# A decoder block on one core: two pooling groups by halves of the tokens, and a pooled half of the output projection, beside the last pair of heads

## The chip, the core and the metric

One core of a Trainium2 chip runs the whole kernel in one launch. TensorE (PE) multiplies, with its weight loads as a queue of their own (PEld); VectorE (DVE), ScalarE (ACT) and GpSimd (POOL) do the elementwise work; SyncE (SP) issues most DMAs. The metric is the device time in microseconds, median of several runs; smaller is better.

## The reference, cut to what matters

One layer over 1024 tokens of width 1024, in float32:

```python
h = x @ w_in                              # [pool 512 | q 512 | k 512 | v 512 | forget gate 8]
# pool: channel group g (128 channels, g = 0..3), windows 2, 4, 8, 16
d = trailing_mean(u, window[g]) - u       # fewer tokens at the start
pool = (d @ pool_w[g]) * pool_scale
# attention: 8 heads of 64, causal, bias c_t - c_s with c = cumsum(log sigmoid(f))
attn = softmax(q k^T / 8 + c_t - c_s) v
x = LayerNorm(alpha * x + concat(pool, attn) @ w_out)
x = LayerNorm(alpha * x + relu(x @ w_mlp1)**2 @ w_mlp2)
```

## The kernel before

Every float32 matrix product is made of three matmuls of rounded parts: each operand is split into a rounded high part (a CAST on ScalarE) and the rest (a subtraction on VectorE); `three` issues high x high (L83), high x low (L84) and low x high (L85). `split` (L71, L72) makes the parts, `load_w` loads a 128-column block of weights and splits it.

The order of the work on each engine comes from a scheduler: the program is written as generators, and the scheduler orders the instructions of each engine by its own estimates, within the written dependencies; tile pools with a fixed number of buffers per tag ("S" 3, "U" 2, "B" 14, "Q" 10, "A" 9 in SBUF; "s" 3, "pt" 2, "pv" 1, "mm" 2 banks of PSUM) release and hand on buffers. Each engine and each DMA queue then works in order.

The stages around the change:

- Values and gates, then the pooling groups. `pool_group` projects one group of 128 channels for all 1024 tokens: for each half of the tokens (`c`, 512 wide) 8 blocks of x by `three`, 24 matmuls; the window sums by doubling on VectorE over 1024 columns, the difference `d`, its split. `pool_linear` multiplies by the group's 128 x 128 matrix (3 matmuls for each half), scales on ScalarE and stores to `mix_dram`. Groups 3, 2 and 1 (`EARLY`) run so before the attention.
- Attention, four pairs of heads, 8 blocks a pair. A block of 256 queries (`m` = 0 to 3) of one head: `att_probs` makes the scores (L370, L371, and L373 for the mask in the last pair), VectorE adds the gate row and takes the running minimum (L376), ScalarE the exponential (L378). `att_values`, one block later, transposes (L398), splits (L399 on ScalarE, L400 on VectorE) and multiplies with V (L414). L419 and L420 take the result out, to `mix_dram`; `row_scales` stores the reciprocal row sums to `rin_dram`.
- Filler: `fillstep`, called between the blocks, runs pieces of a generator at a rate. For the first three pairs that is the next pair's projection of q and k; for the last pair it is `last_fill`: group 0 whole.
- The output projection. `wo` holds `w_out` in 8 blocks of 128 rows: three are loaded and split here, five were split earlier and lie in `wo_dram`. For each 256 tokens (`m`) the mixture is read back from `mix_dram` in two halves, the pooled one (channel blocks 0 to 3) and the attention one (4 to 7, multiplied with the row scales), and split. For each tile of 128 tokens `t` 48 matmuls of 512 columns (8 blocks, 2 halves of the output, `three`), then the norm and the transposes for the MLP.
- The MLP, from about 400 us to the end, which the change leaves alone.

```python
fill.update(gen=gen, credit=0.0, rate=pieces / over)   # pieces of a generator over `over` calls of fillstep
```

## Time and profile before

| | us |
|---|---|
| median of 3 runs | 1043.03 |
| lowest and highest run | 1040.76, 1044.09 |
| span of the profiled execution, first to last instruction | 1039.2 |
| PE busy | 1016.9 (98%) |
| weight loads (PEld) busy | 844.9 (81%) |
| VectorE busy | 760.8 (73%) |
| ScalarE busy | 510.7 (49%) |
| GpSimd busy | 142.7 (14%) |

The profile has the span of one execution and no time of its own for it; the median of the runs is 3.8 us above the span. A busy PE is the union of pipelined matmuls: one of 512 columns is shown 0.39 us long, though the next starts 0.23 us after it. The granted TensorE clock is full over the whole span.

### The profile page before, as it was taken

Reading aid. Unit: us, or ns where it says so; the run is one execution under the profiler, and the core shown is the slowest. Engines: PE = TensorE matmul, PEld = TensorE weight load, DVE = VectorE, ACT = ScalarE, POOL = GpSimd, SP = SyncE. Lnnn points to the kernel's source line nnn. Section 1 sums busy time; section 2 is a strip of 40 time slices with the busy share of each in tenths; the row PEclk is TensorE's granted clock in tenths of the full one; section 3 lists DMA queues with packets and bytes.
Section 4 is the critical chain, followed back from the end, with each engine's and each line's share of the span. In section 5 each row is a group of like instructions: output and inputs, shape, how many; then the busy total and the mean of one; then the engine's idle time right before and its main releaser. Section 6 shows DMA issues by size and latency. Waiting matters only on the chain.

```text
span 1039.2 us, 14092 instructions
## 1 busy us (share of the span) xinstructions
PE 1016.9 (98%) x4976; PEld 844.9 (81%) x4976; DVE 760.8 (73%) x1303; ACT 510.7 (49%) x820; POOL 142.7 (14%) x246
## 2 busy tenths in 40 slices
PE   9999999999989999999999999999999999999996
PEld 9988888878777888887888888888788888888884
DVE  4776678777786887988878778788875566566547
ACT  4623566666673321676766766768531221122152
POOL 0200112111000021113122122120100000000057
PEclk9999999999999999999999999999999999999998
DMA  9702211111376642139667566566999888878753
GB/s 358 274 27 87 98 52 52 34 50 54 101 250 207 195 148 102 62 134 349 266 240 276 215 262 263 227 231 221 346 308 305 283 264 281 271 228 271 242 186 121
DMA packets 114678, 206.29 MB, mean 199 GB/s; under 512 B 9576, under 2 KB 77992, under 8 KB 114608
## 3 DMA queue, kind: packets, MB, share of 16 engines
q1 hardware_dynamic: 96896, 141.82, 41.1%
q0 software_dynamic: 17280, 62.92, 15.6%
q8 instruction: 39, 0.64, 0.2%
q10 hardware_dynamic: 432, 0.66, 0.2%
q14 instruction: 31, 0.25, 0.1%
HBM read 132.42 MB, written 72.94 MB: 198 GB/s over the span
## 4 chain that ended last, share of the span: by engine, by line
PE 50%; issue 4%; DVE 3%; DMA 1%; POOL 1%; SPq 0%; ACT 0%; DVEq 0%; POOLq 0%
PE s L981 15%; PE pv L981 8%; PE s L627 8%; PE mm L627 6%; PE pt L627 6%; PE pv L627 4%; PE pt L981 2%; PE mm L981 2%; DMA hid_dram<-A 1%; DMA A<-hid_dram 1%; DVE B L72 1%; POOL hid_dram L752 0%; POOL A L620 0%; SPq L960 0%; DVE A L750 0%
## 5 line engine op out<-in xcount | busy, mean ns | idle before, releaser
L71 ACT CAST B<-S 128x1024 fp32r<-128x1024 f32 (+1 forms) x79 | 69.0, 885 | 168.8 <-DMA S<-in_w_dram 61.2
L627 PE MATMUL s<-B,Q 128*128 128x512 f32 x480 | 113.5, 389 | 0.2 <-ACT B L71 0.2
L627 PEld LDWEIGHTS s<-B,Q 128*128 128x128 f32 x480 | 90.0, 188 | 19.3 <-ACT B L71 0.6
L72 DVE TENSOR_TENSOR B<-S,B 128x1024 fp32r<-128x1024 f32 (+1 forms) x79 | 79.4, 1013 | 29.9 <-ACT B L71 29.8
L981 PE MATMUL s<-B,Q 128*128 128x512 f32 x390 | 94.8, 389 | 0.0
L71 ACT CAST Q<-S 128x1024 fp32r<-128x1024 f32 x52 | 54.7, 1052 | 64.0 <-PE s L627 17.0
L981 PEld LDWEIGHTS s<-B,Q 128*128 128x128 f32 x390 | 73.2, 188 | 15.6
L981 PE MATMUL s<-B,A 128*128 128x512 f32 x333 | 83.1, 394 | 1.2 <-DMA A<-hid_dram 1.2
L752 POOL DMA_DIRECT2D hid_dram<-A x90 | 48.3, 542 | 217.1 <-ACT A L749 174.7
L981 PEld LDWEIGHTS s<-B,A 128*128 128x128 f32 x333 | 62.4, 188 | 15.9 <-DMA A<-hid_dram 1.9
L72 DVE TENSOR_TENSOR Q<-S,Q 128x1024 fp32r<-128x1024 f32 x52 | 63.4, 1219 | 15.6 <-ACT Q L71 15.5
L627 PE MATMUL pt<-B,Q 128*128 128x512 f32 x300 | 71.6, 389 | 0.0
L627 PE MATMUL mm<-B,Q 128*128 128x512 f32 x300 | 71.6, 389 | 0.0
L414 PE MATMUL pv<-A,B 128*128 128x256 f32 x320 | 64.0, 299 | 3.0 <-DVE A L400 1.6
L627 PEld LDWEIGHTS mm<-B,Q 128*128 128x128 f32 x300 | 56.3, 188 | 11.7
L627 PEld LDWEIGHTS pt<-B,Q 128*128 128x128 f32 x300 | 56.3, 188 | 11.7
L414 PEld LDWEIGHTS pv<-A,B 128*128 128x128 f32 x320 | 49.6, 188 | 19.0 <-ACT A L399 8.8
L400 DVE TENSOR_TENSOR A<-pt,A 128x512 fp32r<-128x512 f32 (+1 forms) x80 | 49.2, 634 | 18.2 <-ACT A L399 17.7
L378 ACT ACTIVATE A<-A,nm 128x1024 f32<-128x1024 f32 (+7 forms) x64 | 49.8, 778 | 20.0 <-DVE nm L376 19.6
L750 DVE TENSOR_TENSOR A<-A,A 128x1024 f32<-128x1024 f32 x45 | 53.6, 1220 | 0.0
L399 ACT CAST A<-pt 128x512 fp32r<-128x512 f32 (+1 forms) x80 | 41.7, 540 | 18.5 <-PE pt L398 17.3
L981 PE MATMUL pv<-B,Q 128*128 128x512 f32 x204 | 50.3, 390 | 0.0
(407 smaller groups left out, 2309.7 us busy)
## 6 DMA issues: line engine op xcount, KB each, us to landing
hid_dram<-A POOLq DMA_DIRECT2D x105, 512.0 KB, 4.0
S<-in_w_dram SPq DMA_DIRECT2D x62, 512.0 KB, 3.7
Q<-hid_dram SPq DMA_DIRECT2D x101, 256.0 KB, 5.1
A<-hid_dram SPq DMA_DIRECT2D x79, 256.0 KB, 4.5
S<-in_wuqk_dram SPq DMA_DIRECT2D x12, 512.0 KB, 3.3
wo_dram<-Q POOLq DMA_DIRECT2D x10, 512.0 KB, 4.0
B<-wo_dram SPq DMA_DIRECT2D x10, 512.0 KB, 4.1
A<-ncf_dram SPq DMA_DIRECT2D x8, 512.0 KB, 3.9
```

The source lines that it names most:

```text
L71: nc.scalar.copy(hi, src)
L72: nc.vector.tensor_tensor(lo, src, hi.bitcast(F32), ALU.subtract)
L378: nc.scalar.activation(pt[:, :nk], pt[:, :nk], AF.Exp, bias=nm, scale=-1.0, accum_out=rsum[h][:, i : i + 1])
L399: nc.scalar.copy(tt[:, 0, ev], tp[:, ev])
L400: nc.vector.tensor_tensor(tt[:, 1, ev], tp[:, ev], tt[:, 0, ev].bitcast(F32), ALU.subtract)
L414: nc.tensor.matmul(ov, V[j][:, h].rearrange("p s d -> p (s d)"), tt[:, s, a:b], start=(j == 0 and s == 0), stop=(j == 2 * m + 1 and s == 1),)
L627: nc.tensor.matmul(dst, b[x][:, k], A[a][y][:, k], start=first and k == 0 and i == 0, stop=k == H - 1 and i == 2, skip_group_check=not first,)
L750: nc.vector.tensor_tensor(x, x, hi.bitcast(F32), ALU.subtract)
L752: nc.gpsimd.dma_start(hid_dram[self.u, :, i, AT[name] : AT[name] + 2 * CH], part.rearrange("p q n t -> p (q n t)"))
L981: nc.tensor.matmul(dst, h[:, p_], w[q_], start=first and u == self.us[0] and j == 0, stop=u == self.us[-1] and j == 2, skip_group_check=no ...
```

## The change

`EARLY` loses group 1, which joins group 0 in the filler of the last pair, now by halves of the tokens: `late_group(g, c, w)` projects 512 tokens, copies them out on ScalarE, forms the window sum on GpSimd (group 0: a subtraction of neighbours; group 1: an addition of neighbours, a scale-and-add on VectorE, another addition, and a few columns at the seams) and splits the result. The factor 1/window moves into the scale. `late_linear(g, c)` mixes and stores one half; it loads and splits the group's matrix each time. The filler then loads the output weights in two lots, reads the pooled half of the first mixture back and begins the output projection of token tile 0 with its 24 matmuls of blocks 0 to 3. It is 44 pieces over 24 steps, before 18 over 14. The output projection finishes what has been begun.

```diff
-EARLY, LATE = (3, 2, 1), (0,)
+EARLY, LATE = (3, 2), (1, 0)
...
+    def late_group(g, c, w):
+        x = slot("Q", [2, CH], F32)
+        u, s = x[:, 0], x[:, 1]
+        dst = bank("mm")
+        for _ in proj(dst, c, w):
+            yield
+        nc.scalar.copy(u, dst)
+        add = nc.gpsimd.tensor_tensor
...
+        if g == 0:
+            d, mx = s, u
...
+            add(d[:, 1:], u[:, :-1], u[:, 1:], ALU.subtract)
+        else:
+            d, mx = u, s
+            add(s[:, 1:], u[:, 1:], u[:, :-1], ALU.add)
...
+            nc.vector.scalar_tensor_tensor(d, u, -4.0, s, ALU.mult, ALU.add)
+            add(d[:, 2:], d[:, 2:], s[:, :-2], ALU.add)
...
+        y = slot("Q", [2, CH])
+        split(y[:, 0], y[:, 1], d)
+        pooled[g, c] = (y, mx)
+
+    def late_linear(g, c):
+        st = slot("S", [P], F32)
+        nc.sync.dma_start(st, poolw[:, g])
+        pw = slot("U", [2, P])
+        split(pw[:, 0], pw[:, 1], st)
+        y, mx = pooled.pop((g, c))
+        dst = bank("mm")
+        three(dst, (pw[:, 0], pw[:, 1]), (y[:, 0], y[:, 1]), True, True)
+        nc.scalar.activation(mx, dst, AF.Copy, scale=scales[:, g : g + 1])
+        nc.sync.dma_start(mix_dram[2 * c : 2 * c + 2, :, g, :]..., mx...)
...
     def last_fill():
...
+        ws = [load_w(wuqk[g]) for g in LATE]
+        old = None
+        for c in range(NCH):
+            for g, w in zip(LATE, ws):
+                yield from late_group(g, c, w)
+                if old:
+                    late_linear(*old)
+                    yield
+                old = (g, c)
+            if c == 0:
+                load_output_weights(0, 4)
+        load_output_weights(4, KT)
+        late_linear(*old)
+        yield
+        yield from pooled_half(0)
...
+    def pooled_half(t):
+        mixture(t // 2, 0)
+        sums[t] = [bank("mm") for n in range(2)]
+        yield from out_proj(t, range(KT // 2))
...
-                gen, pieces, over = last_fill(), (2 * KT + 2) * len(LATE), 14
+                gen, pieces, over = last_fill(), (2 * KT + 2) * len(LATE) + 8, 24
...
+            begun = t in sums
+            if not begun:
+                sums[t] = [bank() for n in range(2)]
+            run(out_proj(t, range(KT // 2 if begun else 0, KT)))
```

`load_output_weights`, `mixture` and `out_proj` hold the lines that stood in the output projection before.

Where this puts the instructions, at three places. First PE, from the last mixing matmuls of the pooled groups (destination `mm`, weights in Q and U) on. Before, they stand among the last pair's last scores (`s`), with all of the last two blocks' transposes (`pt<-ident,A`) and values (`pv`) behind them:

```order
L370 MATMUL s_3454<-Q_2390,Q_2391 128x512
L371 MATMUL s_3454<-Q_2390,Q_2392 128x512
L414 MATMUL pv_3392<-A_3394,B_389 128x256 x2
L398 MATMUL pt_3413<-ident_63,A_3273 128x128
L398 MATMUL pt_3413<-ident_63,A_3260 128x128
L398 MATMUL pt_3413<-ident_63,A_3273 128x128
L414 MATMUL pv_3392<-A_3402,B_402 128x256 x4
L431 MATMUL pt_3435<-ident_63,ri_3433 2x128
L370 MATMUL s_3459<-Q_2390,Q_2391 128x512
L371 MATMUL s_3459<-Q_2390,Q_2392 128x512
```

Now PE has the end of group 0's projection of the second half of the tokens (`mm_3336`), and the mixing matmuls of both groups (`mm_3450`, `mm_3473`) around the same block's values:

```order
L85 MATMUL mm_3336<-B_437,B_2910 128x512
L414 MATMUL pv_3397<-A_3407,B_402 128x256 x4
L83 MATMUL mm_3450<-Q_3321,U_3447 128x512
L84 MATMUL mm_3450<-Q_3321,U_3447 128x512
L85 MATMUL mm_3450<-Q_3321,U_3447 128x512
L414 MATMUL pv_3397<-A_3422,B_478 128x256 x4
L431 MATMUL pt_3489<-ident_63,ri_3487 2x128
L370 MATMUL s_3495<-Q_2303,Q_2304 128x512
L83 MATMUL mm_3473<-Q_3442,U_3470 128x512
L371 MATMUL s_3495<-Q_2303,Q_2305 128x512
L370 MATMUL s_3500<-Q_2303,Q_2304 128x384
L84 MATMUL mm_3473<-Q_3442,U_3470 128x512
```

The projection has moved from four blocks ahead of the end to the last block but one, and the mixing of its result stands ten matmuls behind it. From there to the first output matmul PE has only the last scores, then the transposes and values of one block.

Second ScalarE, at the same place. Before, the pooled result's scaling (L302) has the rest of the attention behind it, and the mixture's split (`Q_3628<-S_3626`) comes 12 rows on:

```order
L302 ACTIVATE Q_3323<-mm_3329,psc_76 128x512
L378 ACTIVATE A_3379,rsum_2921<-A_3379,nm_3389 128x1024
L399 CAST A_3414<-pt_3413 128x384
L433 COPY row_3437<-pt_3435 2x128
L378 ACTIVATE A_3440,rsum_2986<-A_3440,nm_3450 128x896
L399 CAST A_3468<-pt_3467 128x512
L419 COPY U_3429<-pv_3392 64x256
L378 ACTIVATE A_3453,rsum_2986<-A_3453,nm_3463 128x1024
L399 CAST A_3476<-pt_3475 128x512
L399 CAST A_3488<-pt_3487 128x512
L399 CAST A_3500<-pt_3499 128x384
L433 COPY row_3523<-pt_3521 2x128
```

Now the copy of the projection (L453), the split of its difference (`Q_3442<-Q_3335`, behind GpSimd) and two scalings (L495) stand there, and the mixture's split (`Q_3522<-S_3520`) has moved ahead of the last cast of its block:

```order
L453 COPY Q_3335<-mm_3336 128x512
L71 CAST Q_3442<-Q_3335 128x512
L495 ACTIVATE Q_3198<-mm_3450,scales_1061 128x512
L419 COPY U_3483<-pv_3397 64x256
L433 COPY row_3491<-pt_3489 2x128
L495 ACTIVATE Q_3335<-mm_3473,scales_1061 128x512
L378 ACTIVATE A_3494,rsum_2899<-A_3494,nm_3504 128x896
L399 CAST A_3536<-pt_3535 128x512
L378 ACTIVATE A_3507,rsum_2899<-A_3507,nm_3517 128x1024
L399 CAST A_3544<-pt_3543 128x512
L399 CAST A_3562<-pt_3561 128x512
L71 CAST Q_3522<-S_3520 128x1024
```

A new wait on GpSimd is thus queued ahead of the last exponentials.

Third SyncE's queue. Before, from the last output weights (`wo_dram`) to the mixture's load:

```order
L511 DMA B_3613<-wo_dram 128x1024
L421 DMA mix_dram<-U_3355 64x256
L516 DMA Q_3618<-in_g_dram 128x1024
L303 DMA mix_dram<-Q_3323 128x4x256
L434 DMA rin_dram<-row_3437 2x128
L516 DMA Q_3620<-in_b_dram 128x1024
L778 DMA S_3626<-mix_dram 128x1024
```

Now:

```order
L532 DMA B_3457<-wo_dram 128x1024
L532 DMA B_3462<-wo_dram 128x1024
L532 DMA B_3463<-wo_dram 128x1024
L532 DMA B_3462<-wo_dram 128x1024
L532 DMA B_3463<-wo_dram 128x1024
L496 DMA mix_dram<-Q_3198 128x2x256
L421 DMA mix_dram<-U_3483 64x256
L496 DMA mix_dram<-Q_3335 128x2x256
L434 DMA rin_dram<-row_3491 2x128
L540 DMA S_3520<-mix_dram 128x1024
```

The two row loads (`g`, `b`) have moved behind the mixture's load, and the output weights' loads have moved close ahead of it.

102 lines of the change are left out of this document (67 added, 35 removed).

## The prediction

> **What bounds the kernel now.** I read the page first, then the windows over the stages, then the stretch between the last pair of heads and the output projection in the timelines of TensorE, ScalarE and SyncE's queue.
>
> ```profile
> span 1039.2 us, 14092 instructions
> PE 1016.9 (98%) x4976; PEld 844.9 (81%) x4976; DVE 760.8 (73%) x1303; ACT 510.7 (49%) x820; POOL 142.7 (14%) x246
> PEclk9999999999999999999999999999999999999998
> GB/s 358 274 27 87 98 52 52 34 50 54 101 250 207 195 148 102 62 134 349 266 240 276 215 262 263 227 231 221 346 308 305 283 264 281 271 228 271 242 186 121
> ```
>
> TensorE (PE) is busy almost throughout, at full granted clock, so only its holes can be won. Moving matmuls from one dense place to another wins nothing. The windows show where the holes are. Their columns are busy time and, in brackets, instructions of each engine.
>
> ```profile
> core 0: us, PE busy (x) PEld busy (x) DVE busy (x) ACT busy (x) POOL busy (x), PEclk, DMA share, GB/s
> 80.00:100.00 20.00, 20.00 (x90) 16.52 (x89) 13.24 (x20) 6.93 (x10) 0.52 (x1) 1.00 0.22 79
> 268.60:285.20 16.60, 16.29 (x97) 12.71 (x96) 13.83 (x39) 13.24 (x34) 1.15 (x4) 1.00 0.35 115
> 285.20:294.70 9.50, 9.50 (x61) 8.12 (x60) 7.14 (x22) 5.06 (x14) 0.42 (x2) 1.00 0.82 289
> 294.70:306.50 11.80, 10.25 (x65) 8.06 (x63) 10.95 (x27) 8.89 (x19) 0.31 (x1) 1.00 0.64 231
> 306.50:315.80 9.30, 6.62 (x47) 5.23 (x46) 5.10 (x15) 6.42 (x15) 0.62 (x2) 1.00 0.71 234
> 315.80:321.50 5.70, 5.70 (x36) 4.80 (x37) 4.64 (x7) 2.73 (x6) 0.00 (x0) 1.00 0.80 225
> 321.50:340.00 18.50, 18.50 (x83) 15.20 (x82) 13.96 (x22) 6.16 (x8) 0.00 (x0) 1.00 0.61 181
> ```
>
> The last pair's attention runs from 268.6 to about 321.5. At 285.2 to 294.7 it is mixed with matmuls of pooling group 0 and weight loads (PEld) fill 8.12 of 9.50 us, 0.855. At 294.7 the projection of group 0 is used up and the share falls to 0.683, then 0.562. From 315.8 on the output projection fills it again. At the pace of the filled window the three thin stretches would take 12.71/0.855 = 14.9 us for 16.6, 8.06/0.855 = 9.4 for 11.8 and 5.23/0.855 = 6.1 for 9.3: room of 1.7, 2.4 and 3.2 us, 7.3 in all. That is the most this change can win.
>
> [...] By PE's own busy column the room would be 0.3 + 1.6 + 2.7 = 4.5 us.
>
> **The moved matmuls.** A dense stretch of 512-wide matmuls gives their price:
>
> ```profile
> 330.15 0.39 PE L84 MATMUL s<-B,Q 128*128 128x512 f32 x1
> ...
> 335.14 0.39 PE L85 MATMUL s<-B,Q 128*128 128x512 f32 x1
> ```
>
> These are the first and last of 23, so 4.99/22 = 0.227 us each. Group 1's 48 projection and 6 mixing matmuls, 54 x 0.227 = 12.25 us, leave a dense place (80 to 100 us, no idle time) and land in the last pair. The pooled half of token tile 0, 24 matmuls or 5.4 us, leaves the dense output projection. Both are zero in the sum; what counts is which holes they fill.
>
> The first attention scores then come 12.25 us earlier. What must be there is the table of gate sums:
>
> ```profile
> 90.77 0.38 SPq L347 DMA_DIRECT2D A<-ncf_dram  x1
> 110.33 0.39 PE L370 MATMUL s<-Q,Q 128*128 128x512 f32 x1
> A<-ncf_dram SPq DMA_DIRECT2D x8, 512.0 KB, 3.9
> ```
>
> Issued at 90.8 and landed 3.9 us later, it is ready before 98.1. I take zero, at worst 1 us, since six matmuls fewer lie beside the first head's scores.
>
> **The first two thin stretches.** Filler goes from 18 pieces of three matmuls over 14 steps (1.3 a step) to 44 over 24 (1.8 a step). In the changed order the projection of group 0's second half of tokens ends right before the last block's scores, so the stretch at 294.7 is filled: -2.4 us. In the stretch at 268.6 filler was there already and becomes 40% denser; I take a third of its room, -0.6 (bounds 0 and -1.7).
>
> **The last thin stretch.** Here the changed order still has no filler: between the last mixing matmul of the pooled groups and the first output matmul stand only scores, transposes and values of the last two heads. What sets its length is a round trip through DRAM:
>
> ```profile
> 299.40 0.33 SPq L511 DMA_DIRECT2D B<-wo_dram  x1
> 304.16 0.39 PE L85 MATMUL mm<-Q,U 128*128 128x512 f32 x1
> 304.13 1.27 ACT L302 ACTIVATE Q<-mm,psc 128x512 f32<-128x512 f32 x2 [0.26 <-PE mm L85]
> 305.42 0.37 SPq L303 DMA_DIRECT2D mix_dram<-Q  x1
> 308.34 0.32 SPq L778 DMA_DIRECT2D S<-mix_dram  x1
> 314.69 1.05 ACT L71 CAST Q<-S 128x1024 fp32r<-128x1024 f32 x1 [1.50 <-DMA S<-mix_dram]
> 315.79 0.50 PE L83 MATMUL s<-B,Q 128*128 128x512 f32 x1 [1.22 <-ACT Q L71]
> DMA to landing us min/median/max: 2.2/4.1/6.1
> S<-mix_dram SPq DMA_DIRECT2D x8, 512.0 KB, 6.1
> Q<-in_wout_dram SPq DMA_DIRECT2D x5, 512.0 KB, 10.2
> ```
>
> PE's last mixing matmul ends at 304.5, the first output matmul starts at 315.8: 11.3 us, of which the load waits 2.9 us to be issued after the store and takes 6 us. In the changed order it stands one small store behind, so it is issued some 0.9 us after: the trip shrinks to 9.3 us with the same landing. PE's work inside it shrinks too. Values and transposes cost
>
> ```profile
> 284.54 0.86 PE L414 MATMUL pv<-A,B 128*128 128x256 f32 x6
> 285.24 0.27 PE L431 MATMUL pt<-ident,ri 128*2 128x128 f32 x1
> 293.94 1.03 PE L398 MATMUL pt<-ident,A 128*128 128x128 f32 x8
> 294.73 0.48 PE L370 MATMUL s<-Q,Q 128*128 128x512 f32 x1
> ```
>
> 0.70/6 = 0.117 and 0.79/8 = 0.099 us each. Before, 26 values, 29 small ones and 4 wide scores stand there, 6.8 us, and 4.5 us are empty. Afterwards 12, 18 and 5: 4.3 us, and 9.3 - 4.3 = 5.0 us are empty, 3.0 if the load lands after 4.1 us (the median of this tensor's transfers there, stores among them), 1.1 at the shortest of 2.2. I take the middle of 4.1 and 6.1, since no row load is issued right ahead of it any more: 4.0 us empty, -0.5 (bounds -3.4 and +0.5).
>
> **New waits.** Group 0's second half has a chain between its last projection matmul and its mixing matmul: ScalarE's copy, a one-column and a 511-wide subtraction on GpSimd, ScalarE's rounding. Prices:
>
> ```profile
> L272 ACT COPY Q<-mm 128x512 f32<-128x512 f32 x2 | 1.1, 575 | 0.0
> L581 POOL TENSOR_TENSOR A<-A,S 128x512 f32<-128x512 f32 x2 | 2.5, 1260 | 1.1 <-ACT A L580 1.1
> L675 POOL TENSOR_TENSOR S<-S,S 128x512 f32<-128x512 f32 x1 | 1.8, 1797 | 56.2 <-DVE Q L72 56.2
> L620 POOL TENSOR_TENSOR A<-A,Q 128x512 f32<-128x512 f32 x2 | 4.0, 2015 | 22.9 <-DVE Q L616 22.9
> L400 DVE TENSOR_TENSOR A<-pt,A 128x512 fp32r<-128x512 f32 x15 | 10.0, 687 | 2.7 <-ACT A L399 2.7
> L784 DVE TENSOR_TENSOR S<-S,S 128x1024 f32<-128x1024 f32 x1 | 1.2, 1219 | 0.0
> L71 ACT CAST Q<-S 128x1024 fp32r<-128x1024 f32 x2 | 2.1, 1051 | 1.6 <-DMA S<-mix_dram 1.5
> ```
>
> A subtraction costs 1.26 us with VectorE quiet and 1.8 to 2.0 beside it; I take 1.7, plus 0.2 for the single column. 0.58 + 0.2 + 1.7 + 0.58 = 3.1 us, against 8 values, 4 wide matmuls and a small one on PE in between, 1.9 us. PE is in order, so the last block's scores queue behind: +1.1 (bounds +0.4 and +2.0). The other three half-groups have 40 and more PE rows between projection and mixing and cost PE nothing, though ScalarE and VectorE stand still for a microsecond or two each, queued in front of the previous head's exponentials and evictions; that cover is the filler itself.
>
> [...]
>
> Last, the attention half of the first mixture. Its multiplication (1.22) and rounding (1.05) now stand ahead of the last head's final casts on VectorE and ScalarE; before, they stood behind them. The 24 pooled matmuls have to cover that and the last head's own chain: +1.0 (bounds 0 and 2.5). The three output weight blocks that are split earlier (1.05 and 1.22 us each) are the same work in a stretch that is 18 us longer; zero.
>
> **Sum.** -2.4 - 0.6 - 0.5 + 1.1 + 1.0 = -1.4 us on the span of 1039.2: 1037.8. The runs' median is 1043.03, 3.8 us over the span, so 1041.6. Everything from the second output tile on stands in the same order on PE and moves up as a block.
>
> **Rivals.** *The round trip closes too.* If the mixture lands in 4.1 us, the denser filler takes 1.2 of the first room, and GpSimd and the tail cost their lower ends, the sum is -1.2 - 2.4 - 1.5 + 0.4 + 0.2 = -4.5: 1038.5. For it: the load no longer has a row load and a second mixture load beside it from the start. Against it: the median of 6.1 over the eight mixture loads.
>
> *The mixture load lands late.* Before, the last output weight block was issued at 299.4, 9 us ahead of the mixture load. Now four such loads of 512 KB wait for the buffers that the last projection frees, and go out on SyncE's queue some 5 us ahead of it. Five loads that went out together took 10.2 us to land. At 10.2 in place of my 5.1 the hole at the first output matmul grows by 5.1 us: -1.4 + 5.1 = +3.7, 1046.7. It decides from a landing of 9.6 us on. Against it: four loads are 2.1 MB, and in its fullest slice the span moved 358 GB/s, so 6 us of transfer are mostly over when the mixture's turn comes.
>
> *Filling does nothing*, as VectorE is 10.95 of 11.80 us busy at 294.7. Then -2.4 falls away: +1.0, 1044.0. Against it: group 0's 1024-wide steps are what filled VectorE, and they go to GpSimd or halve.
>
> **How the numbers follow.** A measurement tells 0.3%, 3.1 us, from no change. My forecast has 0.36, the idle filler 0.10, both within: 0.46. The closed round trip has 0.34, the late landing (with whatever else holds the tail up) 0.20. All lower ends together give 1.7 + 2.4 + 3.4 - 0.4 = -7.1, all upper ends about +5; the range 1037.0 to 1047.0 leaves out less than 2 in 10. The likeliest case alone spans 1039.9 to 1044.
>
> **What would show it.** Right: weight-load share near 0.85 from the last pair's start to its last scores, then a hole of 3 to 5 us on PE ended by ScalarE's rounding of the mixture; a wait of about 1 us at the last mixing matmul ended by ScalarE behind GpSimd; no hole before the first scores near 98. Wrong: waits of ScalarE or VectorE on GpSimd that reach PE earlier, a landing beyond 9 us, or a hole in the output projection.

## The result, and the profile after

The changed kernel takes 1047.3 us (median of 5 runs, 1045.0 to 1050.3), the kernel before, on the same chip, 1041.7 (5 runs, 1040.5 to 1044.1): the ratio is 1.0058, interval 1.004 to 1.0077. It is slower by 5.7 us, 0.6%. Forecast was 1041.6, which is 1.4 us less than the 1043.03 that the prediction counted from.

First the page of the changed kernel, then the windows over the last pair of heads, before and after. Columns are as in the prediction.

```profile
span 1043.8 us, 14122 instructions
PE 1018.6 (98%) x4976; PEld 843.9 (81%) x4976; DVE 758.2 (73%) x1300; ACT 511.4 (49%) x824; POOL 149.6 (14%) x264
```

```profile
268.60:294.70 26.10, 25.79 (x156) 20.83 (x155) 20.97 (x60) 18.30 (x48) 1.56 (x5) 1.00 0.52 178
294.70:315.80 21.10, 16.87 (x110) 13.29 (x108) 16.05 (x39) 15.31 (x32) 0.94 (x3) 1.00 0.68 232
```

```profile
255.50:294.90 39.40, 36.99 (x209) 29.52 (x209) 27.17 (x71) 25.85 (x60) 8.19 (x21) 1.00 0.35 113
294.90:314.70 19.80, 17.15 (x99) 12.94 (x97) 12.13 (x31) 13.55 (x27) 2.10 (x6) 1.00 0.84 273
...
272.80:280.40 7.60, 5.84 (x34) 4.11 (x32) 5.19 (x9) 3.93 (x10) 1.43 (x3) 1.00 0.67 225
...
294.90:304.70 9.80, 9.76 (x59) 7.86 (x57) 6.07 (x16) 6.14 (x13) 1.20 (x4) 1.00 0.89 291
304.70:314.70 10.00, 7.40 (x43) 5.08 (x41) 6.06 (x15) 7.41 (x14) 0.90 (x3) 1.00 0.78 256
```

Over the whole last pair, up to the first output matmul, weight loads fill 34.12 of 47.2 us before (0.72) and 42.46 of 59.2 after (0.72): the added filler has made the pair longer, not denser. The prediction's sign of being right was a share near 0.85. The stretch that had run dry is filled (294.9 to 304.7: 0.80), but a new thin one stands at 272.8 to 280.4 (0.54), where VectorE and ScalarE are idle a third to a half of the time as well. PE's own timeline has what it waits for (in brackets, the idle time and what ended it):

```profile
273.71 0.51 PE L414 MATMUL pv<-A,B 128*128 128x256 f32 x2 [0.44 <-ACT A L399]
276.05 0.74 PE L414 MATMUL pv<-A,B 128*128 128x256 f32 x4 [0.44 <-DVE A L400]
280.74 0.50 PE L83 MATMUL mm<-Q,U 128*128 128x512 f32 x1 [1.22 <-ACT U L71]
...
305.74 0.50 PE L83 MATMUL mm<-Q,U 128*128 128x512 f32 x1 [0.62 <-ACT Q L71]
...
314.71 0.50 PE L83 MATMUL mm<-B,Q 128*128 128x512 f32 x1 [0.93 <-ACT Q L71]
```

Only the last two of these waits were forecast. The first output matmul starts 1.1 us earlier than before (315.79). The first transposes of the output projection start 1.1 us later, and from there to the fifth tile's another 3.3 us are lost. The transposes before:

```profile
340.81 0.60 PE L600 MATMUL pv<-ident,A 128*128 128x128 f32 x4
...
352.59 0.60 PE L600 MATMUL s<-ident,A 128*128 128x128 f32 x4
...
376.15 0.60 PE L600 MATMUL s<-ident,A 128*128 128x128 f32 x4
```

and after (L704 is the same line):

```profile
341.92 0.63 PE L704 MATMUL pv<-ident,A 128*128 128x128 f32 x4 [0.41 <-issue]
...
366.21 0.63 PE L704 MATMUL pv<-ident,A 128*128 128x128 f32 x4 [0.32 <-DVE A L659]
...
379.33 0.63 PE L704 MATMUL s<-ident,A 128*128 128x128 f32 x4 [1.01 <-DVE A L659]
...
380.89 0.63 PE L704 MATMUL mm<-ident,A 128*128 128x128 f32 x4 [0.93 <-DVE A L659]
```

L659 is the norm's last step on VectorE. It is late because the mixtures' multiplications by the row scales stand in VectorE's order ahead of it, and wait. Before (L784) and after (L546):

```profile
331.77 1.23 DVE L784 TENSOR_TENSOR S<-S,S 128x1024 f32<-128x1024 f32 x1
342.28 1.23 DVE L784 TENSOR_TENSOR S<-S,S 128x1024 f32<-128x1024 f32 x1 [1.87 <-DMA S<-rin_dram]
353.50 1.23 DVE L784 TENSOR_TENSOR S<-S,S 128x1024 f32<-128x1024 f32 x1 [0.74 <-DMA S<-rin_dram]
```

```profile
337.30 1.23 DVE L546 TENSOR_TENSOR S<-S,S 128x1024 f32<-128x1024 f32 x1 [1.88 <-DMA S<-rin_dram]
350.04 1.23 DVE L546 TENSOR_TENSOR S<-S,S 128x1024 f32<-128x1024 f32 x1 [2.21 <-issue]
361.97 1.23 DVE L546 TENSOR_TENSOR S<-S,S 128x1024 f32<-128x1024 f32 x1 [3.91 <-issue]
```

They come 5.5, 7.8 and 8.5 us later. Where the bracket says "issue", the input that was out is the row scales as well: the last load for the middle one, issued at 342.93 (below), took 7.0 us to land, and the view of these loads' line (L545) lists 5.8 us of waits by L546, 1.88 and 3.91. VectorE cannot make that up: in its windows (third pair of columns) it loses 4 us in the first and is full in the next two, at the end of which PE is idle 2 us.

```profile
350.00:362.00 12.00, 12.00 (x59) 10.02 (x58) 7.94 (x14) 3.49 (x6) 0.00 (x0) 1.00 0.67 198
362.00:374.00 12.00, 11.68 (x56) 9.39 (x55) 11.82 (x21) 5.28 (x8) 0.17 (x1) 1.00 0.52 178
374.00:386.00 12.00, 10.05 (x49) 7.96 (x48) 11.79 (x17) 3.02 (x5) 6.12 (x4) 1.00 0.40 138
```

SyncE's queue after shows the loads that the multiplications wait for (L545) behind a store of the last head, behind mixture loads that hold the queue until a buffer is free (7.68 us from the first issue to the end of the second, at 338.87; the multiplication that frees one ends at 338.53), and around the norm's stores (L660):

```profile
329.27 0.49 SPq L421 DMA_DIRECT2D mix_dram<-U  x1
329.81 1.29 SPq L545 DMA_DIRECT2D S<-rin_dram  x2
331.19 7.68 SPq L540 DMA_DIRECT2D S<-mix_dram  x2
341.18 0.58 SPq L545 DMA_DIRECT2D S<-rin_dram  x1
341.85 1.03 SPq L660 DMA_DIRECT2D x_dram<-A  x2
342.93 0.58 SPq L545 DMA_DIRECT2D S<-rin_dram  x1
```

Before, the last head's store was issued at 322.45 and the second mixture's row scales at 324.34. In each of the five executions the time is 1.74 to 1.82 us above the span; the span was 1045.6 in their median, so the profiled one (1043.8) is a short one. Of the 5.7 us between the medians the two profiles show 4.6; where the rest is lost they do not tell.

### The profile page after: what moved, and what is told of

Read it like the earlier page. It is cut to its first block, busy times and chain, and to the rows that moved or that the text cites. A ratio compares the mean times of both kernels' runs of the same rounds, so it can differ in the third digit from the quotient of the medians.

```text
span 1043.8 us, 14122 instructions
## 1 busy us (share of the span) xinstructions
PE 1018.6 (98%) x4976; PEld 843.9 (81%) x4976; DVE 758.2 (73%) x1300; ACT 511.4 (49%) x824; POOL 149.6 (14%) x264
## 4 chain that ended last, share of the span: by engine, by line
PE 52%; DVE 3%; DMA 1%; issue 1%; ACT 1%; SPq 0%; POOL 0%; DVEq 0%; POOLq 0%; ACTq 0%
PE s L1074 15%; PE s L731 9%; PE pv L1074 8%; PE pt L731 6%; PE mm L731 6%; PE pv L731 4%; PE pt L1074 2%; PE mm L1074 2%; DMA hid_dram<-A 1%; DVE B L72 1%; DMA A<-hid_dram 1%; DMA S<-in_w_dram 0%; SPq L1053 0%; DVE A L854 0%; POOL hid_dram L856 0%
## 5 line engine op out<-in xcount | busy, mean ns | idle before, releaser
L1074 PEld LDWEIGHTS s<-B,Q 128*128 128x128 f32 x390 | 73.2, 188 | 15.8
L414 PE MATMUL pv<-A,B 128*128 128x256 f32 x320 | 63.7, 298 | 4.2 <-DVE A L400 2.3
L414 PEld LDWEIGHTS pv<-A,B 128*128 128x128 f32 x320 | 50.5, 188 | 20.4 <-ACT A L399 8.5
L378 ACT ACTIVATE A<-A,nm 128x1024 f32<-128x1024 f32 (+7 forms) x64 | 49.7, 777 | 22.3 <-DVE nm L376 22.0
L83 PE MATMUL mm<-B,B 128*128 128x512 f32 x144 | 59.3, 412 | 0.0
L85 PE MATMUL mm<-B,B 128*128 128x512 f32 x144 | 57.1, 397 | 0.0
L84 PE MATMUL mm<-B,B 128*128 128x512 f32 x144 | 57.1, 396 | 0.0
```

The lines of the kernel that those rows point to most:

```text
L83: nc.tensor.matmul(dst, a[0], b[0], start=first, stop=False)
L84: nc.tensor.matmul(dst, a[0], b[1], start=False, stop=False)
L85: nc.tensor.matmul(dst, a[1], b[0], start=False, stop=last)
L378: nc.scalar.activation(pt[:, :nk], pt[:, :nk], AF.Exp, bias=nm, scale=-1.0, accum_out=rsum[h][:, i : i + 1])
L414: nc.tensor.matmul(ov, V[j][:, h].rearrange("p s d -> p (s d)"), tt[:, s, a:b], start=(j == 0 and s == 0), stop=(j == 2 * m + 1 and s == 1),)
L1074: nc.tensor.matmul(dst, h[:, p_], w[q_], start=first and u == self.us[0] and j == 0, stop=u == self.us[-1] and j == 2, skip_group_check=no ...
```

## The experiments

Each edit is to the changed kernel, unless it says otherwise. The table has, for each run, the ratio to the kernel before, the mean granted clock over its timed executions, and three marks of the profiled execution on PE: first output matmul, first transposes (the same work is done by then in all of them) and the time from those to the fifth tile's transposes. In e3 the order of the tiles' transposes differs.

Two cautions. The marks are those of one execution, and its span can lie off the median of its version: e7's is 1040.3 where the median is 1043.0, the changed kernel's 1043.8 where it is 1045.6. So a difference of marks under some 3 us is a hint, and the ratio decides. And each edit lets the scheduler order the engines anew, so versions differ by more than the edited lines.

| run | ratio, interval | clock | output | transposes | to fifth |
|---|---|---|---|---|---|
| before | 1 | 0.997 | 315.8 | 340.8 | 47.1 |
| changed | 1.0058, 1.004 to 1.0077 | 0.997 | 314.7 | 341.9 | 50.4 |
| e1 | 1.0039, 1.0026 to 1.0052 | 0.997 | 315.3 | 343.3 | 48.9 |
| e2 | 1.0145, 1.012 to 1.0169 | 0.993 | 315.6 | 346.1 | 57.0 |
| e3 | 1.0092, 1.0078 to 1.0106 | 0.992 | 309.0 | | |
| e4 | 1.0018, 1.0006 to 1.003 | 0.995 | 307.4 | 340.4 | 48.4 |
| e5 | 1.006, 1.0045 to 1.0075 | 0.996 | 314.7 | 341.3 | 53.1 |
| e6 | 1.0065, 1.0051 to 1.0079 | 0.996 | 315.9 | 343.1 | 51.6 |
| e7 | 1.0042, 1.0027 to 1.0057 | 0.995 | 310.6 | 338.9 | 50.2 |
| e8 | 1.0065, 1.005 to 1.008 | 0.993 | 306.7 | 338.6 | 55.8 |
| e9 | 1.0068, 1.0051 to 1.0084 | 0.993 | 319.8 | 348.0 | 47.1 |
| e10 | 1.0048, 1.0036 to 1.006 | 0.993 | 313.9 | 344.8 | 47.4 |
| e11 | 1.004, 1.0027 to 1.0052 | 0.993 | 311.0 | 345.4 | 47.1 |
| e12 | 1.0034, 1.0022 to 1.0046 | 0.996 | 315.6 | 340.6 | 49.7 |
| e13 | 1.0053, 1.0039 to 1.0066 | 0.995 | 306.2 | 338.7 | 53.7 |
| e14 | 1.0022, 1.0013 to 1.0032 | 0.996 | 306.5 | 341.5 | 47.0 |
| e15 | 1.0039, 1.0026 to 1.0051 | 0.995 | 314.2 | 344.6 | 47.4 |
| e16 | 1.0045, 1.0032 to 1.0057 | 0.995 | 315.1 | 344.1 | 50.0 |
| e17 | 1.0008, 0.9995 to 1.0021 | 0.996 | 307.3 | 339.1 | 49.3 |
| e18 | 1.0015, 1.0006 to 1.0025 | 0.996 | 308.0 | 343.1 | 47.4 |

### Which part of the change costs: e1, e4, e7

e1, no pooled output matmuls beside the attention (their mixture is still read early; the second edit keeps the later tiles' banks):

```diff
         mixture(t // 2, 0)
-        sums[t] = [bank("mm") for n in range(2)]
-        yield from out_proj(t, range(KT // 2))
+        yield
...
-    rr[0] = 4
+    rr[0] = 2
```

> The changed kernel, with the pooled half of the first mixture still read early, but its 24 output matmuls run where they stood before, behind the attention. Theory L (late last head): those 24 matmuls stand between the values of the last head but one, so the last head ends 6.5 us later, the row scales of the next mixtures are read later, and VectorE, which works in order, keeps the norms behind the multiplication that waits for them; PE's transposes wait, 3.3 us in all. Then this run has no such waits, the last values end near 322 us instead of 329, and the span falls by about 3 us to 1041 (ratio to the kernel before 1.002 to 1.003). Rival P (the loss is made in the last pair, by ScalarE and VectorE standing behind GpSimd and the output weights' split): the last pair is untouched, so the span stays at 1044 and the ratio at 1.005 to 1.006.

The last values do end early (PE's last of L414 starts at 321.9, in the changed kernel at 328.0), and the short waits at the first and third tile's transposes (0.41 and 0.32 us) go. Those at the fourth's stay: 0.44 and 0.94 us, where the changed kernel has 1.01 and 0.93. Theory L gave 3 us, the runs show 2.0, with intervals that overlap, and by the fifth tile's transposes the two profiled executions are level (392.2 and 392.3). The last of the multiplications came at 361.8 here too: its row scales were late for another reason. The second mixture's show which. Their load goes out at 328.50, 4.2 us later than before, though the last head's store is out at 323.05. The first mixture's multiplication is 4.2 us late as well (324.91 after 320.75), and the load goes out as VectorE's split of that mixture ends (328.48): it waits for a buffer S that the first mixture frees.

e4, group 1 back ahead of the attention:

```diff
-EARLY, LATE = (3, 2), (1, 0)
+EARLY, LATE = (3, 2, 1), (0,)
```

> The changed kernel with group 1 back ahead of the attention: group 0 alone by halves of the tokens, the pooled half of tile 0 still beside the last pair, 26 pieces over 24 steps. Theory L: the pooled matmuls still stand in front of the last head's values and the transposes still wait about 3 us; the last pair has thinner filler (room of some 2 us more), so the time is no better than the changed kernel, ratio 1.004 to 1.008. Rival P, in the form that group 1's chain of GpSimd and VectorE steps is what costs: the waits at 272.9, 275.2 and 278.8 us go, 2.1 us, and the ratio falls to 1.002 to 1.004, with the transposes' waits gone too if they come from the last pair's delay.

The rival came nearest. Moving group 1 costs 0.40% of the 0.58% (intervals apart), some 4 us; halves of the tokens and the pooled half together cost the remaining 0.18%. Which part of the move costs (group 1's chain, the denser filler, the new order), this run does not tell.

e7, the late groups' steps on VectorE:

```diff
-        add = nc.gpsimd.tensor_tensor
+        add = nc.vector.tensor_tensor
```

> The changed kernel, with the late groups' sums and differences on VectorE instead of GpSimd. Theory P (the GpSimd chains cost part of it): the waits of PE for ScalarE and VectorE at 272.9 and 275.2 us, 0.44 each, and of the mixing matmul at 305.7, 0.62, go: 1.5 to 2 us of holes, ratio 1.004. Rival: at the thin stretches VectorE is busy nearly throughout, so some 5 us of added steps there (ten of 512 columns at 0.5 to 0.7 us) stand ahead of the scores' minimum and the casts, and the time stays or grows: ratio 1.005 to 1.007. Theory N expects the transposes' waits to stay either way.

As theory P had it. Between 270 and 282 us PE has no wait left, and the pooled output matmuls begin at 310.6, the first transposes 3.0 us earlier than in the changed kernel, so the last pair is where GpSimd's chains cost. The runs show 1.7 us only, and intervals that overlap, so the time alone does not prove it; the mean clock has fallen from 0.997 to 0.995, some 2 us of a span. The transposes' loss stays, as theory N expected.

### The output weights: e3, e6

e3 loads all output weights behind the last projection, e6 the first half of them one step later:

```diff
e3              if c == 0:
e3 -                load_output_weights(0, 4)
e3 -        load_output_weights(4, KT)
e3 +        load_output_weights(0, KT)
...
e6 +                if (g, c) == (1, 1):
e6 +                    load_output_weights(0, 4)
e6                  old = (g, c)
e6 -            if c == 0:
e6 -                load_output_weights(0, 4)
```

> The changed kernel, with all output weights loaded in one lot behind the last projection instead of half of them between the two halves of the tokens. Theory W (a part of the loss): ScalarE's split of an output weight block, which waits for its load, stands ahead of the pool matrix's split, and PE waits 1.22 us for that at 278.8 us, 1.4 us of hole. Then that wait goes and the span falls by 1.2 to 1.5 us (ratio 1.004), unless the weights now land too late and a hole of the same kind appears at the first output matmul. Theories L and P without it: no change, ratio 1.005 to 1.006.

> The changed kernel, with the first half of the output weights loaded one step later, behind the mixing of group 0's first half of tokens and not ahead of it. Theory W: of the changed kernel's loss 1.4 us come from the split of an output weight block that stands on ScalarE ahead of the pool matrix's split, and waits for its load; the run with all weights at the end had no such wait but lost 7.8 us to a late first mixture. Here only the place of one lot moves, so the wait at 278.8 us goes and nothing comes in its place: span 1042.4, ratio 1.004 to 1.0045. Rival: the split waits elsewhere in ScalarE's queue just as long; ratio 1.0055.

In both the wait of 1.22 us at the pool matrix's split went and nothing was won, against theory W. In e3 the first output matmul comes early (309.0), and a hole of 7.79 us opens behind the last values, at the attention half of the first mixture:

```profile
336.05 0.79 PE L83 MATMUL mm<-B,Q 128*128 128x512 f32 x1 [7.79 <-ACT Q L71]
...
333.69 1.23 DVE L546 TENSOR_TENSOR S<-S,S 128x1024 f32<-128x1024 f32 x1 [8.20 <-DMA S<-rin_dram]
```

What is late there is not the mixture's load, as in the prediction's second rival (it was issued at 321.20 and had landed by 326.8), but the row scales. The second of their two loads was issued at 326.04, right behind the last head's store (325.52).

### The norms on VectorE: e2, e5, e8

e2 multiplies on GpSimd. e5 queues the multiplication and the split of mixture m on VectorE behind the last step of tile m - 1's norm. e8 is e5 with e4's edit.

```diff
e2 -            nc.vector.tensor_tensor(mf, mf, rb, ALU.mult)
e2 +            nc.gpsimd.tensor_tensor(mf, mf, rb, ALU.mult)
...
e5 -                mixture(m, half)
e5 +                with tc.issue_after(norms[m - 1].done) if m and half else nullcontext():
e5 +                    mixture(m, half)
```

> The changed kernel, with the mixture's multiplication by the row scales on GpSimd instead of VectorE. Theory L: the norms no longer stand behind the multiplication, and GpSimd has nothing else there: the waits of PE's transposes (2.2 us listed, 3.3 us of holes) go, though the last head still ends at 329 us; span about 1041, ratio 1.002 to 1.003. A 1024-wide multiplication takes GpSimd 2.5 to 4 us where VectorE took 1.2, so if the mixture itself is what comes late, PE waits at the output matmuls instead and nothing is won. Rival P: no change, ratio 1.005 to 1.006.

> The changed kernel, with the second, third and fourth mixture's multiplication and its split queued on VectorE behind the norm of the first, second and third token tile; PE's order is the same to the row. The theory, sharper after the first runs (call it N): what costs the 3.3 us at PE's transposes is VectorE's order alone. The multiplication waits for the row scales' load (1.9, 2.2 and 3.9 us at 337, 350 and 362 us) and the norm's last steps stand behind it, though the mixture is not needed for ten more us. The first two runs fit it: with the last head early the multiplication still waited 3.8 us at 361.8; and with GpSimd multiplying, the product's split stood in the norm's way instead. Then here the waits of PE's transposes go and the span falls by 2.5 to 3.3 us: 1040.5 to 1041.3, ratio 1.002 to 1.003. Rival R (the ring of three buffers S is what is late): a later multiplication frees its buffers later, the loads of the next mixture shift, and PE waits at the output matmuls: ratio 1.005 or more.

> Group 0 alone by halves of the tokens and the pooled half of tile 0 beside the last pair (the run with group 1 back ahead of the attention, ratio 1.0018, with 1.3 us of holes left at the transposes), and the mixtures' multiplications queued behind the norms as in the run before. Theory N: those 1.3 us go and the ratio falls to 1.000 to 1.001. If the rest of its loss, 4.2 us of waits for the first mixture's split at the first pooled output matmuls, is what counts: 1.0018 as before. Theory R: slower than 1.0018.

e2 is 9 us slower than the changed kernel, some 4 of them by the clock (0.993 for 0.997): the product's split stands on VectorE where the multiplication stood, and the multiplication takes 2.66 us for 1.23.

```profile
341.12 2.66 POOL L546 TENSOR_TENSOR S<-S,S 128x1024 f32<-128x1024 f32 x1 [14.14 <-DMA S<-rin_dram]
...
358.92 1.23 DVE L72 TENSOR_TENSOR Q<-S,Q 128x1024 fp32r<-128x1024 f32 x1 [6.54 <-ACT Q L71]
```

In e5 the first three tiles' transposes are 11.8 us apart, as before, so the order is what held those norms; then the fourth and fifth come 13.7 and 15.8 us on, 3.4 of the latter by the clock. The last mixture's multiplication is at 365.8 there, 3.8 us later than in the changed kernel, which is theory R's half of it. The clock falls at 379.4 (below). e8 repeats it with one group. Nothing is won by the order alone while the row scales are late.

### The row scales' queue: e9 to e12, e15

The row scales are loaded from GpSimd's queue: all four in e9, and in e10 (with e7's edit), e11 (with e7's and e4's) and e12 (an edit to the kernel before); all but the first in e15 (with e7's).

```diff
e9  -                nc.sync.dma_start(rb[e * HD ...
e9  +                nc.gpsimd.dma_start(rb[e * HD ...
...
e15 +                (nc.gpsimd if m else nc.sync).dma_start(rb[e * HD ...
```

> The changed kernel, with the row scales of the mixtures loaded from GpSimd's queue instead of SyncE's, where GpSimd has little to do. Theory Q (queue, the form that is left after eight runs): in the changed kernel the row scales' loads stand in SyncE's queue behind the last heads' late stores and behind the norms' stores, so the multiplications of mixtures 1 to 3 come 5.5, 7.8 and 8.5 us later than before; VectorE, in order, stands idle some 8 us behind them, is full for the next 24 us (11.8 of 12) and so delivers the norms late; PE loses 3.3 us at the transposes. Taking the norms ahead alone only moved the wait on, since the loads stayed late. Here the loads go out as soon as a buffer is free: tr. waits gone or under 1 us, span 1040.5 to 1041.3, ratio 1.002 to 1.003. Rival (the ring of three buffers S sets the pace, wherever the loads are issued): ratio 1.005 to 1.006.

> As the run before, and the late groups' elementwise steps on VectorE as well. The two losses are in different places (the last pair; the output projection), so they should add: the first output matmul at 310.6 as with VectorE alone, and the output projection at the kernel before's pace (47.1 us from the first to the fifth tile's transposes, 50.2 in that run): span 1037.2, ratio 0.999 to 1.0005. Rival (ring): 1.004, as with VectorE alone.

> Group 0 alone by halves of the tokens, its steps on VectorE, and the row scales' loads from GpSimd's queue; group 1 stays ahead of the attention. If moving group 1 is worth nothing once its chain costs nothing (its matmuls only change places), this is as fast as the run with both groups: 0.998 to 1.0005. If group 1 is needed as filler, 1.000 to 1.002: this run keeps 2 to 4 us of wait for the first mixture's split at the first pooled output matmuls, as with one group on GpSimd.

> The kernel before, with the row scales' loads from GpSimd's queue: a control. In it the transposes never wait, so theory Q expects no change: 0.999 to 1.001. If the queue for these loads is worth something by itself, it is faster than 0.997, and what it brings to the changed kernel says nothing on the change.

> The changed kernel with the late groups' steps on VectorE, the round trip as it was, and the row scales of the second to fourth mixture from GpSimd's queue. Theory Q: 2 to 3 us less than with VectorE alone (1.0042): 1.0015 to 1.0025, the output projection at 47.1 to 47.5 us between the first and fifth transposes instead of 50.2. Theory H adds that the clock's loss at the first output matmul stays. Rival (GpSimd's queue): 1.004 to 1.005.

The mark of the output projection bears theory Q out: in all four changed kernels it is 47.1 to 47.4 us, as before. The times do not. By the first transposes each is 5 to 6 us behind the run that it is to be compared with (the changed kernel, e7, e4, e7), and a front that is late by itself gives the row scales more time, so the mark alone does not prove the theory. Of that delay the clock is 3.4 us in e9 and e11 and 1.7 in e10 (below).

In e15 the profiles show where it comes from, and most of it is not the queue. PE's order is that of e7 up to the first transposes. At 300 us ScalarE's split of a pool matrix waits for a buffer U, by the trace for the landing of a store of 64 KB from it (e7, then e15):

```profile
296.54 0.30 ACT L71 CAST U<-S 128x128 fp32r<-128x128 f32 x1 [0.21 <-DMA mix_dram<-U]
300.17 0.30 ACT L71 CAST U<-S 128x128 fp32r<-128x128 f32 x1 [3.40 <-DMA mix_dram<-U]
```

PE waits 2.60 us behind it, and GpSimd's queue issues its first row scales 27 us later, at 327.2. e16, which leaves the row scales alone, has the same wait (3.57 us). Another 1.70 us is a wait at the first transposes themselves, outside the mark. There the scheduler has put the second mixture's multiplication ahead of the first tile's norm on VectorE, and it waits 4.38 us; e14 and e18 below have the same, with 1.66 and 1.61 us.

The control, e12, is slower by 0.34%, so the edit has a price in the kernel before too. It is not paid at the front (first transposes at 340.6, before 340.8) but in the output projection, 49.7 us for 47.1. The second and the last multiplication wait 4.32 and 2.38 us for their row scales there, before 0 and 0.74. Whether the queue or the new order does that stays open. e10 (both groups) and e11 (group 0 alone) have 1.0048 and 1.004, with intervals that overlap: with its steps on VectorE, moving group 1 shows no price of its own.

### The round trip: e13, e14, e16, e17, e18

e13, with e7's edit: the pooled half of the first mixture, which needs the first half of the tokens only, is read back once those are mixed, so the round trip through DRAM is over long before the pooled output matmuls. e14 adds e15's edit. e16 is e7 with e1's edit. e17 is e4 with the early mixture, e18 adds e15's row scales to it.

```diff
+                if (g, c) == (1, 1):
+                    mixture(0, 0)
                 old = (g, c)
...
     def pooled_half(t):
-        mixture(t // 2, 0)
```

> The changed kernel with the late groups' steps on VectorE (ratio 1.0042) and the pooled half of the first mixture read back as soon as both groups' first half of tokens is mixed, one half of the tokens earlier; it needs no more than that. Theory H (hole and clock): at the first output matmul stands a hole of 5 us with few matmuls, made by the round trip of the last mixing through DRAM, and in eight of twelve profiles with such a hole (PE less than 0.4 busy for 3.4 us) the granted clock fell to 0.5 for 3.4 or 6.8 us right behind it. Without the round trip the output matmuls follow the last scores: first output matmul 3 us earlier, clock 0.997 instead of 0.993 to 0.996, span down by 4 to 5 us from 1043.0 to 1038.5, ratio 0.999 to 1.000. Rival: the hole is the last heads' chain itself (exponential, casts, transposes), which stays: ratio 1.003 to 1.004.

> As the run before, and the row scales of the second to fourth mixture loaded from GpSimd's queue (the first from SyncE's as before, so that it does not compete with the first mixture). If the 3 us at the transposes come from the late row scales, and what the earlier run with all four from GpSimd's queue lost it lost at the first mixture, this is 2 to 3 us faster than the run before: ratio 0.996 to 0.998, faster than both kernels. Rival (GpSimd's queue is slow by itself: the kernel before with it was 1.0034): no better than the run before.

> The changed kernel with the late groups' steps on VectorE and without the pooled output matmuls ahead of the last head (they run behind the attention). The pooled half cost 1.9 us with GpSimd (1.0058 against 1.0039); if it costs that by itself, this is 1.0015 to 1.0025. If with VectorE the filler is worth its place (theory H: fewer matmuls in the hole make the hole longer), this is 1.0045 or slower.

> Group 0 alone by halves of the tokens on GpSimd (ratio 1.0018, with 4.2 us of PE's waits for the first mixture's split at the first pooled output matmuls), and the pooled half of the first mixture read back one half of the tokens earlier. Those 4.2 us were the round trip; without it the granted clock no longer falls there (mean 0.995 against 0.997 before, 2 us) and the time comes to 0.998 to 1.0005 of the kernel before. Rival: as with both groups, the output projection gives it back, since the last head still ends late: 1.001 to 1.003.

> As the run before, and the row scales of the second to fourth mixture from GpSimd's queue. If the output projection's loss is the late row scales, with one group as with two, this is 1 to 3 us faster than the run before: 0.996 to 0.999. If the front is as fast as it can be with two groups (1.0022) and group 1's move is worth nothing, it is 1.000 to 1.0025.

In e13 the first output matmul comes 4.4 us earlier than in e7 and the first transposes 0.2: the output matmuls only changed places with the last heads' values, whose chain is what lasts. That was e13's rival, though the time is above its range (1.0053): the output projection takes 3.5 us longer than in e7, 1.7 of them by the clock. e14 against e13 is the cleanest case of the late row scales, as PE's order is the same up to the first transposes. The multiplications come 1.6, 4.4 and 6.0 us earlier than in e13 (335.16, 348.13, 360.33),

```profile
333.59 1.23 DVE L548 TENSOR_TENSOR S<-S,S 128x1024 f32<-128x1024 f32 x1 [1.83 <-DMA S<-rin_dram]
343.78 1.23 DVE L548 TENSOR_TENSOR S<-S,S 128x1024 f32<-128x1024 f32 x1 [1.09 <-issue]
354.38 1.22 DVE L548 TENSOR_TENSOR S<-S,S 128x1024 f32<-128x1024 f32 x1 [0.88 <-issue]
```

the output projection falls from 53.7 to 47.0 us (1.7 of the 6.7 is the clock in e13), and the ratio from 1.0053 to 1.0022, intervals apart. It is not the 0.997 expected: the first transposes are 2.8 us later than in e13, 1.66 of them by the wait behind the multiplication described above. The fifth tile's come 3.9 us earlier. e16 is at e7's time (1.0045 and 1.0042): with VectorE the pooled half shows neither cost nor gain, against the first of its two forecasts and on the edge of the second. e17, at 1.0008 with 1 inside the interval, is the best version, and no faster than the kernel before; e18 does not improve on it. No run beat the kernel before.

## Why the prediction was wrong

- **First scores: right.** They start at 99.0 us (forecast 98) with no wait. The last pair starts at 255.5 us, before at 268.5, so up to there the whole 12.25 us are won; what is lost is lost later.
- **Thin stretches, -2.4 and -0.6: the failed step is "cost PE nothing".** The stretch at 294.7 was filled as forecast. But of the half-groups' chains and the output weights' splits I wrote that PE's cover was the filler itself, and of the splits "zero"; what came is 0.44 + 0.44 + 1.22 us of waits at 273.7 to 280.7, and the same density over the pair. With them the first transposes are 2.5 us later than the sum (+1.1 in place of -1.4). The other terms came out a little better than forecast, so these two stretches cost some +1.6 in place of -3.0. That is an estimate: the pair is 11.8 us longer, and of this 12.25 are group 1's matmuls, -1.3 the twelve small ones that moved behind the first output matmul, +0.6 the next term and -1.3 the last stretch. e7 points to the half-groups' chains: with them on VectorE the first output matmul is 4.1 us earlier and the transposes 3.0. e6 shows that taking the 1.22 away by itself was not worth anything. The rival "filling does nothing" missed too, since the stretch that had run dry did fill. That the weight loads' share measures the room, and PE's busy time does not, was my estimate: before, at 285.20 to 294.70, PE reads 9.50 of 9.50 us beside 8.12 us of weight loads, and after, at 294.90 to 304.70, 9.76 of 9.80 beside 7.86.
- **Group 0's second half, +1.1: right in kind**, 0.62 us at 305.74, within the bounds. GpSimd's subtraction (L463, at 304.00) took 1.04 us where the sum had 1.7; the first half's took 1.04 too (276.43), and 0.68 on VectorE in e7 (277.09). The 1.26 us that I gave for a quiet VectorE were not that: beside the first of these steps before (1029.50 to 1030.70) VectorE was busy for 1.06 of 1.20 us. Thirteen matmuls stand between its last projection matmul and its mixing, as the sum counted; the text on the change says ten.
- **The last thin stretch, -0.5: right.** The load went out 1.0 us behind the last store and landed after some 4.4 us, nearer the closed round trip than my 5.1. From the end of the last mixing matmul to the first output matmul it is 7.5 us, where the sum had 9.3 at a landing of 6.1, so 8.3 at its 5.1. That leaves 3.2 us empty for 4.0.
- **The attention half of the mixture ahead of the last head's casts, +1.0:** not singled out by a run. From first output matmul to first transposes it is 2.2 us longer than before, 27.2 for 25.0. Twelve more transposes and values there cost 1.3 us at the sum's prices, so 0.9 is left.
- **"Everything from the second output tile on stands in the same order on PE and moves up as a block": failed, 3.3 us.** PE's order is the same, VectorE's and SyncE's are not. ScalarE and VectorE stood still (5.92 and 5.12 us) while the 24 pooled matmuls ran between the last head but one's values,

```profile
321.11 0.37 ACT L419 COPY U<-pv 64x256 f32<-64x256 f32 x1 [5.92 <-PE pv L414]
```

so the last head's store came 6.8 us later and the row scales' loads of the second to fourth mixture, behind it, 5.4 to 7.7. The norms had 0.9 to 2.3 us to spare before, counted from the last step on a half of a tile to that half's transposes. After, the second tile's has 1.3, the first, third and fourth tile's 0.2 or less. The third's last step before and after:

```profile
361.12 1.41 DVE L555 SCALAR_TENSOR_TENSOR A<-A,rt,Q 128x512 f32<-128x512 f32 x2
365.20 1.41 DVE L659 SCALAR_TENSOR_TENSOR A<-A,rt,Q 128x512 f32<-128x512 f32 x2
```

It is 4.1 us later, and the transposes that need it start 1.8 us later (366.21 after 364.37). e14 shows what late loads cost. e1 shows that the pooled matmuls are only one of the reasons for their being late; the ring of three buffers S is another.

The late mixture load, my slower rival, did not happen in the changed kernel, nor in e3. The forecast's "a hole in the output projection" was the right thing to watch and had no price in it.

## What to carry to other kernels

Ask of every moved block not only what PE does in the hole, but what each in-order engine and queue behind it delivers later: here a store and a load in SyncE's queue decided over norms some 40 us on. Before taking "same order on PE" for "moves as a block", look for steps with only a microsecond or two to spare on the engine that feeds PE. Filler that brings its own chain of steps on other engines can make the stretch longer instead of denser, as it did here (59.2 us for 47.2, weight loads at 0.72 in both). And one profiled execution can lie off the others by more than the effect: compare its span with the median first.

## What the runs showed of the hardware

**The granted clock falls in quanta behind a thin window.** In the profiles of before and after the clock falls to 0.50 only at the end of the span, 4.2 and 4.6 us behind PE's last matmul (at 1033.4 of 1039.2 us and at 1038.6 of 1043.8), which gives their means of 0.997 and 0.998. Between 250 and 420 us it stayed at 1.00 in both; in 10 of the 18 experiments it went to 0.50 there, for 3.4 us or for 6.8. Two such places in e9, by windows (first pair of columns PE, then weight loads; the clock is third from the end):

```profile
279.99:283.40 3.41, 1.60 (x9) 1.13 (x8) 2.36 (x7) 3.20 (x6) 0.00 (x0) 1.00 0.34 128
283.40:286.80 3.40, 3.40 (x11) 2.75 (x10) 2.42 (x9) 1.92 (x5) 0.00 (x0) 0.50 0.22 57
314.12:317.53 3.41, 2.44 (x18) 1.76 (x16) 1.55 (x3) 1.06 (x3) 0.00 (x0) 1.00 1.06 308
317.53:320.95 3.42, 1.19 (x6) 0.99 (x6) 1.21 (x2) 1.57 (x3) 0.00 (x0) 1.00 0.50 204
320.95:324.35 3.40, 3.40 (x12) 2.72 (x11) 2.29 (x4) 1.04 (x1) 0.00 (x0) 0.50 0.75 226
```

Behind the windows with PE busy for 1.60 and 1.19 us of 3.41 the next 3.4 us ran at half clock, which costs some 1.7 us (an estimate: half of 3.4); behind the one with 2.44 they did not. In the other profiles with such a fall, too, it followed wherever PE was busy for 1.6 us or less; between 1.7 and 2.1 it went both ways (e7 1.79 and e10 2.09 fell, e8 1.74 did not), so no sharp bound is shown. The two starts are 37.55 us apart, 11 x 3.414. The longest single wait in the first thin window was 1.8 us.

In e2 three falls start 34.13 and 27.31 us apart, 10 and 8 x 3.413: in both profiles the falls lie on a grid of 3.41 us. And a window need not be idle for one, as the 1.60 us of work above show. By these figures a hole of 2 us can cost 3.7, where it lies in one window and leaves PE 1.4 us of work there, or 2, where it is split in halves between two (an estimate: 2 us, with or without half of 3.4). Versions that gathered their waits in one hole (e8, e10, e11: mean clock 0.993) lost more by it than the changed kernel with many small ones (0.997). This is a part of why executions of one version differ: e7's shortest span, 1040.3, had a mean clock of 0.996, its longest, 1047.1, one of 0.993, which is 3 us of the 6.8.

**Beside GpSimd's sums a norm took 6.2 us in place of 2.8.** After, at the fourth tile (VectorE, then GpSimd; a norm's step over two halves of 512 takes 1.41 us elsewhere):

```profile
373.90 3.47 DVE L656 SCALAR_TENSOR_TENSOR A<-A,mv,Q 128x512 f32<-128x512 f32 x2
...
377.99 2.76 DVE L659 SCALAR_TENSOR_TENSOR A<-A,rt,Q 128x512 f32<-128x512 f32 x2
```

```profile
375.20 1.62 POOL L780 TENSOR_TENSOR U<-S,S 128x512 f32<-128x512 f32 x1
376.79 1.74 POOL L782 TENSOR_TENSOR S<-S 128x512 f32<-128x512 f32 x1
```

That is 3.47 and 2.76 in place of 1.41 each, 3.4 us in all, on the norm whose transposes then waited longest. Not every step is slowed so: before, at 1031.64, the norm's first step on a tile in PSUM (`pt`) took 1.41 us with GpSimd at work for all of it (L582 and L581, 1.26 us each). What decides it no run shows. Before, the same sums ran from 368.8 to 375.7 us, beside a norm that was slowed as well (2.44 and 2.79) and still in time. So the slowing is not new with the change, and some 1 us of it is.
